# Block transposes of 32 by 32 on VectorE in place of TensorE transposes, in a hybrid attention layer

## The chip, the cores and the metric

The kernel runs on one core of one Trainium2 chip. The metric is the device time of one execution in microseconds; the time of a kernel is the median of its runs.

## The reference, cut to what matters

One layer over 2048 tokens of width 1024, all in float32, with RMS norms before and after each of three sub-layers:

```python
h = x
u = rms_norm(h, g_mix_pre)
z = u @ w_in                                   # sliding-window attention and a gated recurrence work on z
y = concatenate([ya, yh]) @ w_out
h = h + rms_norm(y, g_mix_post)
u = rms_norm(h, g_x_pre)
m = rms_norm(mem, g_mem)                       # 256 memory tokens
y = cross_attention(u, m, wq_x, wk_x, wv_x, wo_x)   # 4 heads, softmax over the memory tokens
h = h + rms_norm(y, g_x_post)
u = rms_norm(h, g_ffn_pre)
y = (silu(u @ w_gate) * (u @ w_up)) @ w_down
h = h + rms_norm(y, g_ffn_post)
```

## The kernel before, in words

Every large product is made from two float32r parts of each operand (a rounded part `hi` and the rest `lo = raw - hi`), so one product of 128x128 by 128x512 is three matmuls (lines 1122 to 1124 in `products`). Most products are also cut by Strassen's scheme: a block of two token tiles (2 x 128 tokens) by 1024 columns takes seven products in place of eight (`seven`), with sums and differences of the operands made on VectorE.

The middle of the kernel is `phases`, which runs a list of jobs (`jobs`). The first three are the output projection with the norms around it (`mixed_block`), the scores and the softmax of the cross-attention (`score_block`), and its values and output projection, folded into one matrix (`value_block`). Each has eight blocks, one for every two token tiles (n = 0, 2, ..., 14). After them come the FFN's jobs. Within a job the weights stay in SBUF as split tiles `T`; the tokens of a block are loaded from DRAM, transposed so that features lie on the partitions, by `streamed`, which splits them into tiles `S`. ScalarE makes `hi` and VectorE makes `lo` (`split2`, lines 985 and 988); the sums of the Strassen scheme come from `combine` (line 1097). `streamed` runs two products ahead of TensorE (`upto(need[g + 2])`).

A block is described by its stream, by `out` (what is done with each finished 128x512 part) and by `after`, a generator whose pieces are laid beside the steps of the next block, one piece a step. For a mixed block `after` scales the rows by the norm (line 1529), adds the residual rows x (line 1530), stores them to `h1_d`, takes the next norm's mean squares (line 1476), and then transposes both tiles on TensorE (`transposed`, lines 1381 and 1382: eight transposes of 128x128 into two PSUM banks, each bank copied out by ScalarE) and stores them to `h1t_d`. For a score block `out` makes the exponentials, and `after` divides them by their sums on VectorE (line 1573), transposes them in the same way and stores them to `pt_d`. A value block reads `pt_d` and also ends with transposes, of its own result, which go to `u_d`.

When a job nears its end, the weights of the next are fetched and split beside its last blocks (`half`, `resident`): these are the 128x1024 splits of line 988. Beside the blocks run sums of the weights of a later job (line 1032).

All loads and plain stores are issued by SyncE's queue (SP), in one order (`load`, line 75, and `store`, line 78). Row tiles come from a pool of 12 tiles of 128x1024 (`row_tile`); the raw streamed tiles (`sraw`) from a pool of four, two a block. The order within an engine's queue is set at build time by a scheduler that follows the order of the program's text and simulated times.

Of the kernel before, what the change touches and what calls it, by code (L numbers as in the profile page):

```python
# [11 lines left out]
F32 = mybir.dt.float32  # L12
F32R = mybir.dt.float32r
I32 = mybir.dt.int32
AF = mybir.ActivationFunctionType
# [3 lines left out]
P = 128  # L19
T = 2048  # L20
D = 1024
M = 256
# [7 lines left out]
NT = T // P  # L30
# [18 lines left out]
class Layer:  # L49
# [111 lines left out]
    def run(self):  # L161
        tc, nc, I = self.tc, self.nc, self.I
        self._n = 0
        self.last = {}
        kw = dict(reuse_waits="tile")
        self.z_d = tc.dram_tile([DIN, T], F32, name="z_d")

        self.y_d = tc.dram_tile([NT, P, D], F32, name="y_d")
        self.un_d = tc.dram_tile([KT, P, TB], F32, name="un_d")
        self.h1t_d = tc.dram_tile([NT, P, D], F32, name="h1t_d")  # L170
        self.pt_d = tc.dram_tile([NT, P, D], F32, name="pt_d")
        self.h1_d = tc.dram_tile([T, D], F32, name="h1_d")
        self.h2_d = tc.dram_tile([T, D], F32, name="h2_d")
        self.qk_d = tc.dram_tile([D, D], F32, name="qk_d")
        self.vo_d = tc.dram_tile([D, D], F32, name="vo_d")
        self.u_d = tc.dram_tile([KT, P, T], F32, name="u_d")
        self.h_d = tc.dram_tile([NFF, P, T], F32, name="hid_d")
        self.y2_d = tc.dram_tile([T, D], F32, name="y2_d")
        with (
            tc.tile_pool(name="cst", bufs=1) as self.cst,  # L180
            tc.tile_pool(name="sm", bufs=3, **kw) as self.sm,
            tc.tile_pool(name="edge", bufs=1, side="right") as edge,
        ):
            self.consts()

            for pool in (self.cst, edge):
                nc.gpsimd.memset(pool.tile([P, 24], F32, name="pad"), 0.0)
            with (
                tc.tile_pool(name="gp", bufs=1, **kw) as self.gp,
                tc.tile_pool(name="big", bufs=4, **kw) as self.big,  # L190
            ):
                self.mix()
# [867 lines left out]
        for e in (mybir.EngineType.Activation, mybir.EngineType.DVE):  # L1060
            self.last[e] = next((i for i in reversed(traced) if i.engine == e), None)

    def streamed(self, load, nk, kind, engine=None, tiles=False):


        nc = self.nc
        raw = []
        for j in range(2):
            self._n += 1
            t = self.ts.tile([P, 4, 256], F32, tag="raw", name=f"sraw_{self._n}", bufs=self.raws)  # L1070
            if tiles:
                t = t.rearrange("p k c -> p (k c)").rearrange("p (i c) -> p i c", i=2)
                load(t, j)
                raw.append([t[:, i, :].rearrange("p (k c) -> p k c", k=4) for i in range(2)])
            else:
                t = t[:, :nk, :]
                load(t, j)
                raw.append([t[:, :, i * P:(i + 1) * P] for i in range(2)])
        yield None
        (a11, a21), (a12, a22) = raw  # L1080

        room = []
        if kind == "u":
            t = self.tb.tile([P, 4, 2, 4, P], F32R, tag="T", name="S_u", bufs=3)
            room += [t[:, i] for i in range(4)]

        def made(src, e):
            self._n += 1
            t = room.pop(0) if room else self.ts.tile([P, 2, 4, P], F32R, tag="S", name=f"S_{self._n}", bufs=5)
            t = t[:, :, :nk, :]  # L1090
            self.split2(src, t[:, 0], t[:, 1], engine or e)
            return t

        def combine(a, b, op):
            self._n += 1
            t = self.st_pool.tile([P, 4, P], F32, tag="sum", name=f"sum_{self._n}", bufs=3)[:, :nk, :]
            nc.vector.tensor_tensor(t, a, b, op)
            return t

        if kind in "pqu":  # L1100
            for a, e in ((a11, "P"), (a21, "A"), (a12, "P"), (a22, "P")):
                yield made(a, e)
            return
        yield made(a11, "A")
        s1 = combine(a21, a22, ALU.add)
        yield made(s1, "P")
        s2 = combine(s1, a11, ALU.subtract)
        yield made(s2, "A")
        yield made(combine(a12, s2, ALU.subtract), "A")
        yield made(combine(a11, a21, ALU.subtract), "P")  # L1110
        yield made(a12, "A")
        yield made(a22, "P")
# [260 lines left out]
    def transposed(self, y, t):  # L1373
# [8 lines left out]
            nc.scalar.activation(tv[:, 4 * q:4 * q + 4, :], ps.rearrange("p (j t) -> p j t", j=4), AF.Copy)  # L1382
        return tv

    def store_transposed(self, dst, n, tv):
        self.store(dst[:, :, n * P:(n + 1) * P].rearrange("k p t -> p k t"), tv)

# [79 lines left out]
    def tokens(self, src, n):  # L1467

        return lambda kind: self.streamed(lambda t, j: self.load(
            t, src[n:n + 2, :, 512 * j:512 * j + 512].rearrange("i p c -> p i c")), 4, kind, "A", tiles=True)  # L1470

    def mean_square(self, a, to):

        self._n += 1
        junk = self.st_pool.tile([P, 512], F32, tag="part", name=f"junk_{self._n}", bufs=3)
        self.nc.scalar.activation(junk, a, AF.Square, scale=float(D) ** -0.5, accum_out=to)  # L1476
# [34 lines left out]
    def mixed_block(self, n):  # L1511
        nc = self.nc
        y, x, ss = {}, [], []
# [11 lines left out]
        def after():  # L1525
            r = self.rstds(ss[0])
            s2 = self.small("q_s", 4)
            for i in range(2):
                nc.vector.scalar_tensor_tensor(y[i], y[i], r[:, i:i + 1], self.g_mix_post, ALU.mult, ALU.mult)
                nc.vector.tensor_tensor(y[i], y[i], x[i], ALU.add)  # L1530
                self.store(self.h1_d[(n + i) * P:(n + i + 1) * P, :], y[i])
                yield
            yield
            for i in range(2):
                self.mean_squares(y[i], i, s2)
                yield
            r = self.rstds(s2)
            nc.gpsimd.tensor_scalar(self.r_x[:, n:n + 2], r, 1.0, None, ALU.mult)
            yield
            for i in range(2):  # L1540
                self.transposed(y[i], y[i])
                self.store(self.h1t_d[n + i], y[i])
                yield

        return self.tokens(self.y_d, n), out, after, None
# [1 line left out]
    def score_block(self, n):  # L1547
        nc = self.nc
        p, den = {}, {}
# [18 lines left out]
        def after():  # L1568
            for i in range(2):
                rd = self.small("mc", 4)  # L1570
                nc.vector.reciprocal(rd, den[i])
                for h in range(4):
                    nc.vector.tensor_scalar_mul(p[i][:, h * M:(h + 1) * M], p[i][:, h * M:(h + 1) * M], rd[:, h:h + 1])
                yield
            yield
            yield
            for i in range(2):
                self.transposed(p[i], p[i])
                self.store(self.pt_d[n + i], p[i])
                yield  # L1580

        return self.tokens(self.h1t_d, n), out, after, None

    def value_block(self, n):
        nc = self.nc
        y, ss, u, o = {}, [], {}, {}
# [41 lines left out]
                for i in range(2):  # L1628
                    yield from self.token_sums(u[i], o[i], n - 4 + i)

        return self.tokens(self.pt_d, n), out, after, None

    def hidden_blocks(self, b, f):
        nc = self.nc
# [130 lines left out]
```

## Time and profile before

| | us |
|---|---|
| median of 3 runs | 2568.96 |
| lowest, highest | 2566.59, 2569.04 |
| the profiled execution, its own time | 2568.82 |
| its span, from the first to the last instruction | 2566.8 |

In the views, PE is TensorE, PEld its weight loads, DVE VectorE, ACT ScalarE, POOL GpSimd and SP SyncE's DMA queue. A row of a group of instructions gives the line, engine and operation, what is written from what, the shapes, the count, the busy time in us and the mean duration in ns of one, and then the engine's idle time before them with what ended it. A row of a window gives, for each engine, the busy time in us and in brackets the number of instructions, then the granted TensorE clock as a share, the mean busy share of the 16 DMA engines (it passes 1 where packets wait for each other) and GB/s. A row of waits has the total in us, the count and the longest.

### The profile page before, as it was taken

What the parts mean: (1) busy time and instruction counts of PE and PEld (TensorE: products, weight loads), DVE (VectorE), ACT (ScalarE), POOL (GpSimd) and SP (SyncE); (2) the same over time, 40 slices, a digit from 0 to 9 for tenths busy, and PEclk for the clock granted to TensorE, in tenths of its full rate; (3) what the DMA queues carried; (4) which work ended last, traced back from release to release, by engine and by line L of the source; (5) the groups of instructions that cost most, each with busy time, mean ns of one, the idle gap of its engine ahead of it and who ended that gap; (6) DMA issues with size and microseconds to landing.
All of it is one profiled execution on the core that took longest, in us unless ns stands there. A gap on an engine that the chain in (4) does not pass through costs nothing.

```text
span 2566.8 us, 34858 instructions
## 1 busy us (share of the span) xinstructions
PE 2535.9 (99%) x12326; PEld 2125.3 (83%) x12326; DVE 1753.4 (68%) x2791; ACT 1298.0 (51%) x2715; POOL 358.1 (14%) x540
## 2 busy tenths in 40 slices
PE   9999999999999999999999999999999999999998
PEld 8888888888988888888878888888888888888886
DVE  7785488886556778687875655576666557574756
ACT  5563466665555676576663333353333335443543
POOL 4231334321301111101210000000000000000022
PEclk9999999999999999999999999999999999999999
DMA  6445755765887896666973622253565424464776
GB/s 189 148 164 170 200 164 166 231 197 163 259 280 276 300 323 206 214 214 210 331 246 115 205 91 79 79 204 124 182 201 190 156 99 178 171 190 107 228 173 156
DMA packets 357294, 486.35 MB, mean 189 GB/s; under 512 B 20352, under 2 KB 248704, under 8 KB 357120
## 3 DMA queue, kind: packets, MB, share of 16 engines
q1 hardware_dynamic: 351072, 462.11, 54.6%
q0 software_dynamic: 6048, 22.02, 4.9%
q8 instruction: 97, 1.59, 0.3%
q14 instruction: 77, 0.63, 0.1%
HBM read 317.34 MB, written 166.72 MB: 189 GB/s over the span
## 4 chain that ended last, share of the span: by engine, by line
PE 85%; DMA 5%; DVE 4%; ACT 2%; issue 2%; POOL 1%; SPq 0%; DVEq 0%; POOLq 0%; ACTq 0%
PE psm L1122 24%; PE psm L1123 23%; PE psm L1124 23%; PE psg L158 2%; PE psg L157 2%; PE psg L156 2%; PE pss L1381 1%; DMA u_d<-row 1%; DMA raw<-in_wo_x_dram 1%; DMA y_d<-sg 1%; DMA raw<-in_wv_x_dram 1%; DMA z<-in_w_out_dram 1%; DMA x<-in_w_out_dram 0%; DVE T L988 0%; DVE S L808 0%
## 5 line engine op out<-in xcount | busy, mean ns | idle before, releaser
L1123 PE MATMUL psm<-T,S 128*128 128x512 f32 x2680 | 1042.8, 390 | 1.2 <-DVE T L988 1.1
L1122 PE MATMUL psm<-T,S 128*128 128x512 f32 x2680 | 1036.5, 391 | 4.8 <-ACT part L1137 2.7
L1124 PE MATMUL psm<-T,S 128*128 128x512 f32 x2680 | 1030.0, 390 | 1.5 <-DVE S L988 1.5
L1122 PEld LDWEIGHTS psm<-T,S 128*128 128x128 f32 x2680 | 503.0, 188 | 113.4 <-ACT part L1137 5.6
L1124 PEld LDWEIGHTS psm<-T,S 128*128 128x128 f32 x2680 | 503.1, 188 | 107.3 <-DVE S L988 2.8
L1123 PEld LDWEIGHTS psm<-T,S 128*128 128x128 f32 x2680 | 503.2, 188 | 106.0 <-DVE T L988 3.4
L985 ACT ACTIVATE S<-sum 128x512 fp32r<-128x512 f32 (+1 forms) x370 | 223.7, 620 | 370.7 <-PE psm L1124 272.2
L988 DVE TENSOR_TENSOR S<-sraw,S 128x512 fp32r<-128x512 f32 (+1 forms) x315 | 211.5, 679 | 216.9 <-ACT S L985 213.7
L988 DVE TENSOR_TENSOR S<-sum,S 128x512 fp32r<-128x512 f32 (+1 forms) x388 | 259.5, 678 | 54.2 <-ACT S L985 49.1
L1137 ACT ACTIVATE part<-psm 128x512 f32<-128x512 f32 x285 | 169.1, 598 | 239.3 <-PE psm L1124 217.8
L985 ACT ACTIVATE S<-sraw 128x512 fp32r<-128x512 f32 (+1 forms) x300 | 185.2, 619 | 104.6 <-PE psm L1124 100.1
L1509 POOL DMA_DIRECT2D y_d<-row x16 | 14.1, 879 | 1077.4 <-DVE row L1695 1026.5
L988 DVE TENSOR_TENSOR T<-row,T 128x1024 fp32r<-128x1024 f32 (+1 forms) x112 | 131.3, 1187 | 41.1 <-ACT T L985 38.9
L157 PE MATMUL psg<-u,whi 128*128 128x512 f32 x320 | 127.8, 399 | 0.0
L158 PE MATMUL psg<-u,wlo 128*128 128x512 f32 x320 | 127.1, 397 | 0.0
L156 PE MATMUL psg<-u,whi 128*128 128x512 f32 x320 | 127.0, 397 | 0.0
L1476 ACT ACTIVATE junk<-row 128x512 f32<-128x512 f32 x160 | 99.7, 624 | 36.9 <-DVE row L1498 14.4
L985 ACT ACTIVATE T<-row 128x1024 fp32r<-128x1024 f32 (+1 forms) x112 | 113.7, 1034 | 6.1 <-DMA row<-d_s 3.3
L1646 DVE TENSOR_TENSOR row<-psm,part 128x512 f32<-128x512 f32 x66 | 43.7, 688 | 68.2 <-PE psm L1124 68.2
L1655 DVE TENSOR_TENSOR part<-psm,part 128x512 f32<-128x512 f32 x66 | 43.8, 688 | 60.4 <-PE psm L1124 60.2
L1695 DVE TENSOR_TENSOR row<-psm,part 128x512 f32<-128x512 f32 x72 | 49.1, 688 | 49.0 <-PE psm L1124 48.9
L812 ACT ACTIVATE S<-S,w_mn 128x256 f32<-128x256 f32 (+1 forms) x128 | 63.1, 497 | 34.3 <-DVE w_mn L808 34.0
(364 smaller groups left out, 3629.7 us busy)
## 6 DMA issues: line engine op xcount, KB each, us to landing
sraw<-in_w_gate_dram SPq DMA_DIRECT2D x44, 512.0 KB, 3.6
sraw<-in_w_up_dram SPq DMA_DIRECT2D x44, 512.0 KB, 3.7
hid_d<-row SPq DMA_DIRECT2D x44, 512.0 KB, 2.7
sraw<-hid_d SPq DMA_DIRECT2D x32, 512.0 KB, 3.9
sraw<-in_w_in_dram SPq DMA_DIRECT2D x44, 256.0 KB, 3.5
z_d<-pair SPq DMA_DIRECT2D x20, 512.0 KB, 2.9
raw<-in_w_in_dram SPq DMA_DIRECT2D x20, 512.0 KB, 4.9
z_d<-z SPq DMA_DIRECT2D x20, 512.0 KB, 3.9
```

The lines of the kernel that those rows point to most:

```text
L156: nc.tensor.matmul(ps, ah, bh, start=(i == 0), stop=False)
L157: nc.tensor.matmul(ps, ah, bl, start=False, stop=False)
L158: nc.tensor.matmul(ps, al, bh, start=False, stop=(i == n - 1))
L812: nc.scalar.activation(s[:, r, o:], s[:, r, o:], AF.Exp, bias=mn[:, i:i + 1], scale=-1.0, accum_out=den[:, i:i + 1])
L985: self.nc.scalar.activation(hi, raw, AF.Copy)
L988: self.nc.vector.tensor_tensor(lo, raw, f32(hi), ALU.subtract)
L1122: nc.tensor.matmul(ps, s[:, 0, k, :], t[:, 0, k, :], start=st, stop=False, **kw)
L1123: nc.tensor.matmul(ps, s[:, 0, k, :], t[:, 1, k, :], start=False, stop=False, **kw)
L1124: nc.tensor.matmul(ps, s[:, 1, k, :], t[:, 0, k, :], start=False, stop=sp, **kw)
L1137: nc.scalar.activation(t, ps, AF.Copy)
L1476: self.nc.scalar.activation(junk, a, AF.Square, scale=float(D) ** -0.5, accum_out=to)
L1695: nc.vector.tensor_tensor(d, a, b, ALU.add)
```

## The change

Three things are edited. The transposes of the mixed and score blocks leave TensorE and PSUM: `blocked` makes them with two VectorE instructions for a tile, each of which transposes the sixteen 32x32 blocks of a 128x512 half where they stand among the partitions, and writes into a new row tile. What is left of the transpose, the exchange of whole blocks between partitions, is done by the store: `store_blocked` writes each quarter of 32 partitions with a DMA of its own, 128 KB in pieces of 512 bytes, to its place in DRAM. So four stores take the place of one. The DRAM tiles `h1t_d` and `pt_d` have another shape, and the next job's `streamed` reads them with `blocked=True`: the loads have the same size, and the views that split and combine read are four-dimensional, with runs of 32 elements. The third edit moves the division of the probabilities from VectorE to ScalarE. The value blocks' own transposes stay on TensorE.

```diff
-        self.h1t_d = tc.dram_tile([NT, P, D], F32, name="h1t_d")
-        self.pt_d = tc.dram_tile([NT, P, D], F32, name="pt_d")
+        self.h1t_d = tc.dram_tile([NT, 2, P, 512], F32, name="h1t_d")
+        self.pt_d = tc.dram_tile([NT, 2, P, 512], F32, name="pt_d")
...
-    def streamed(self, load, nk, kind, engine=None, tiles=False):
+    def streamed(self, load, nk, kind, engine=None, tiles=False, blocked=False):
...
+        at = dict(a=4) if blocked else {}
+
+        def formed(t):
+            return t.rearrange("p k (a c) -> p k a c", **at) if blocked else t
+
...
-                raw.append([t[:, i, :].rearrange("p (k c) -> p k c", k=4) for i in range(2)])
+                raw.append([t[:, i, :].rearrange("p (a k c) -> p k a c" if blocked else "p (k c) -> p k c", k=4, **at)
+                            for i in range(2)])
...
-            self.split2(src, t[:, 0], t[:, 1], engine or e)
+            self.split2(src, formed(t[:, 0]), formed(t[:, 1]), engine or e)
...
+            t = formed(t)
             nc.vector.tensor_tensor(t, a, b, op)
...
+    def blocked(self, y):
+
+        t = self.row_tile()
+        for h in range(2):
+            hs = slice(h * 512, (h + 1) * 512)
+            self.nc.vector.transpose(t[:, hs].rearrange("p (b k j) -> p b k j", b=4, k=4),
+                                     y[:, hs].rearrange("p (k b i) -> p b k i", b=4, k=4))
+        return t
+
+    def store_blocked(self, dst, t):
+
+        for a in range(4):
+            self.store(dst[:, :, a * P:(a + 1) * P].rearrange("h (b i) s -> i (h b) s", b=4),
+                       t[a * 32:(a + 1) * 32, :].rearrange("i (g s) -> i g s", g=8))
+
...
+    def blocks(self, src, n):
+
+        return lambda kind: self.streamed(lambda t, j: self.load(
+            t, src[n:n + 2, j].rearrange("i p c -> p i c")), 4, kind, "A", tiles=True, blocked=True)
...
 # mixed_block
-                self.transposed(y[i], y[i])
-                self.store(self.h1t_d[n + i], y[i])
+                self.store_blocked(self.h1t_d[n + i], self.blocked(y[i]))
...
 # score_block
-                    nc.vector.tensor_scalar_mul(p[i][:, h * M:(h + 1) * M], p[i][:, h * M:(h + 1) * M], rd[:, h:h + 1])
+                    nc.scalar.activation(p[i][:, h * M:(h + 1) * M], p[i][:, h * M:(h + 1) * M], AF.Copy,
+                                         scale=rd[:, h:h + 1])
...
-                self.transposed(p[i], p[i])
-                self.store(self.pt_d[n + i], p[i])
+                self.store_blocked(self.pt_d[n + i], self.blocked(p[i]))
...
-        return self.tokens(self.h1t_d, n), out, after, None
+        return self.blocks(self.h1t_d, n), out, after, None
...
 # value_block
-        return self.tokens(self.pt_d, n), out, after, None
+        return self.blocks(self.pt_d, n), out, after, None
```

## The prediction

> **What bounds the kernel now.** I read the page first: the busy shares (its first part), and the chain of work that ended last.
>
> ```profile
> span 2566.8 us, 34858 instructions
> PE 2535.9 (99%) x12326; PEld 2125.3 (83%) x12326; DVE 1753.4 (68%) x2791; ACT 1298.0 (51%) x2715; POOL 358.1 (14%) x540
> ...
> PE 85%; DMA 5%; DVE 4%; ACT 2%; issue 2%; POOL 1%; SPq 0%; DVEq 0%; POOLq 0%; ACTq 0%
> ```
>
> TensorE is busy for 99% of the span and carries 85% of the chain. Taking TensorE work away shortens the kernel as long as the other engines keep up at the new pace. Whether they do has to be read from the two stages that the diff touches, the mixed blocks (about 789 to 955 us) and the score blocks (to about 1143 us). VectorE's timeline gives the period of a block: each mixed block has one pair on line 1529.
>
> ```profile
> 871.60 2.48 DVE L1529 SCALAR_TENSOR_TENSOR row<-row,q_r,g 128x1024 f32<-128x1024 f32 x2 [1.79 <-POOL q_r L1491]
> ...
> 892.45 2.48 DVE L1529 SCALAR_TENSOR_TENSOR row<-row,q_r,g 128x1024 f32<-128x1024 f32 x2 [1.79 <-POOL q_r L1491]
> ```
>
> So next I asked for busy time by windows of that period, 20.85 us, and for TensorE's waits from 780 to 1345 us.
>
> ```profile
> core 0: us, PE busy (x) PEld busy (x) DVE busy (x) ACT busy (x) POOL busy (x), PEclk, DMA share, GB/s
> 871.60:892.45 20.85, 20.85 (x101) 17.43 (x100) 15.80 (x20) 12.95 (x33) 2.49 (x7) 1.00 0.92 322
> 934.15:955.00 20.85, 20.85 (x101) 17.43 (x100) 18.85 (x20) 18.50 (x38) 3.42 (x7) 1.00 0.95 328
> 955.00:975.85 20.85, 20.85 (x100) 17.07 (x98) 17.35 (x23) 15.56 (x34) 3.15 (x6) 1.00 0.67 242
> 975.85:996.70 20.85, 20.85 (x99) 17.34 (x98) 19.53 (x38) 14.79 (x37) 4.54 (x6) 1.00 0.49 162
> 1017.55:1038.40 20.85, 20.85 (x101) 17.42 (x101) 15.68 (x30) 12.31 (x30) 4.11 (x5) 1.00 0.72 224
> 1220.00:1260.00 40.00, 38.49 (x181) 31.46 (x180) 36.43 (x50) 24.75 (x59) 9.67 (x12) 1.00 1.05 329
> ```
>
> ```profile
> PE psm L1124 <- DVE S L988: 1.5, 2, 1.2
> PE psm L1123 <- DVE T L988: 1.1, 2, 0.8
> PE psm L1122 <- ACT T L985: 0.5, 1, 0.5
> ```
>
> The first row is a steady mixed block, the fifth a steady score block; the second to fourth are the change from one job to the next, where the new weights are split. PE is full in all five, at a granted clock of 1.00, and those three waits of 3.1 us in all are the whole list. VectorE has 5.05 us free in the steady mixed block, but only 2.0, 3.5 and 1.3 us in the three at the change. DMA is at 0.92 of its engines in the mixed block. Those are the covers that the change draws on.
>
> **What leaves TensorE.** The transposes go through line 1381, with their copies out of PSUM on line 1382 (the view of one line, and the groups by line); the third view is TensorE's timeline around one tile of them (start, duration).
>
> ```profile
> L1381 PE MATMUL pss<-ident,row x384: 270/272/273, 811.4 to 1331.6; 128*128 128x128 f32 x192
> ...
> L1382 ACT ACTIVATE row<-pss 128x512 f32<-128x512 f32 x96 | 53.1, 594 | 2.1 <-PE pss L1381 1.5 <-DVE part L1655 0.4 <-ACT S L985 0.3
> ...
> 946.90 0.39 PE L1122 MATMUL psm<-T,S 128*128 128x512 f32 x1
> 947.13 0.39 PE L1123 MATMUL psm<-T,S 128*128 128x512 f32 x1
> 947.35 0.39 PE L1124 MATMUL psm<-T,S 128*128 128x512 f32 x1
> 947.58 1.03 PE L1381 MATMUL pss<-ident,row 128*128 128x128 f32 x8
> 948.38 0.48 PE L1122 MATMUL psm<-T,S 128*128 128x512 f32 x1
> 948.69 0.39 PE L1123 MATMUL psm<-T,S 128*128 128x512 f32 x1
> ```
>
> The 272 ns of one transpose is pipelined and not its cost; the starts tell that. Two product matmuls without a transpose start 0.23 us apart (946.90, 947.13, 947.35). From the start at 947.35 to the one at 948.69 lie two of them and the eight transposes: 1.34 - 2 x 0.23 = 0.88 us for a tile of eight. The 384 transposes are 48 tiles, 16 each of the mixed, score and value blocks; the value blocks keep theirs. So 32 tiles x 0.88 = **28.2 us** leave TensorE, all on the path, since PE has no idle time around them. The period of a block becomes 20.85 - 1.76 = 19.09 us. ScalarE loses 64 copies of 0.594 us, 2.38 us a block, off the path.
>
> **What VectorE gets.** The durations of its operations on these tiles, from the groups by line:
>
> ```profile
> L1498 DVE TENSOR_TENSOR row<-psm,part 128x512 f32<-128x512 f32 x21 | 14.4, 685 | 1.1 <-PE psm L1124 1.1
> ...
> L1573 DVE TENSOR_SCALAR row<-row,mc 128x256 f32<-128x256 f32 x64 | 18.4, 349 | 0.4
> ...
> L988 DVE TENSOR_TENSOR S<-sraw,S 128x512 fp32r<-128x512 f32 x50 | 34.0, 685 | 7.0 <-ACT S L985 6.8
> ```
>
> Each tile gets two block transposes of 128x512, four a block of two tiles. No transpose on VectorE stands in the trace. The nearest row of that size is 0.685 us (L1498), and I take it; the bounds are 0.35 us (the row of half the size) and twice the first, 1.37 us. Four cost 2.74 us a block. In the score blocks the eight divisions of 0.349 us leave, 2.79 us, so VectorE stays at 15.7 of 19.09 us there. In the steady mixed block it comes to 15.80 + 2.74 = 18.54 of 19.09 us, 97%: full, but still under TensorE. A block at 19.53 of 20.85 us (94%) went without a wait that shows in PE's busy time, because the split halves are made two products ahead. At the change of job it does not fit: 18.85 + 17.35 + 19.53 = 55.73 us in three blocks, with four transposes more in each of the first two (in the third the new four and the divisions cancel) 61.2 us, against 3 x 19.09 = 57.3. I charge the **3.9 us** over as a TensorE wait on line 988's splits; it is nothing if the two products of lead absorb it, and the place where it would be late next.
>
> The transposed tile is now stored in blocks, so the score and value blocks read it through views with runs of 32 elements, in seven VectorE operations a block (three splits, four differences). The trace shows no such run; the rows above have longer ones, all at 0.685 us. The cost lies between nothing and that price once more (a gain is excluded, since the same 512 elements are read), and I take nothing, because the rows above agree whether they read PSUM, a sum or the streamed tile. The upper end is a rival below. The Trainium skill ("Vector Engine (DVE) Microarchitecture Reference", section 5.2, Measured stream behaviour on trn2) has hops between runs of two or more adjacent words free, which would give the zero; no run here shows it.
>
> **What ScalarE gets.** The eight divisions of a score block. The two nearest rows:
>
> ```profile
> L985 ACT ACTIVATE S<-sum 128x384 fp32r<-128x384 f32 x32 | 16.8, 524 | 29.1 <-PE psm L1124 28.5 <-ACT S L985 0.6
> ...
> L985 ACT ACTIVATE S<-sum 128x512 fp32r<-128x512 f32 x338 | 207.0, 629 | 341.5 <-PE psm L1124 243.7 <-issue 96.3 <-ACT S L985 1.0
> ```
>
> 128 columns fewer save 105 ns, so 256 columns take about 0.42 us (between 0.35, VectorE's price, and 0.52): 8 x 0.42 - 2.38 = 1.0 us more, 13.3 of 19.09 us. What is queued behind them on ScalarE is line 985's halves; 5.8 us stay free. The transposes of these tiles come three steps after the divisions, about 8 us, so VectorE does not stand waiting for them.
>
> **What the DMA queue gets.** One store of 512 KB becomes four of 128 KB.
>
> ```profile
> L78 SPq DMA_DIRECT2D h1t_d<-row x16: 319/333/553, 822.0 to 976.7; - x16
> ...
> SPq L78 <- ACT row L1382: 62.9, 23, 7.5
> ...
> L78 SPq DMA_DIRECT2D u_d<-row x16: 360/388/870, 1171.0 to 1332.5; - x16
> ...
> DMA to landing us min/median/max: 3.2/6.4/10.6
> ...
> qd<-z_d SPq DMA_DIRECT2D x64, 128.0 KB, 3.4
> ```
>
> SP issues 3 x 32 = 96 instructions more, at 0.33 to 0.39 us (the rows of h1t_d and u_d): 2.0 to 2.3 us a block. SP already waits at these stores for the copies (62.9 us between 788 and 1142), and now waits for VectorE instead; the streamed loads stand behind, but they are issued a whole block ahead. The bytes do not change; at the shorter period the share of 0.92 becomes 0.92 x 20.85 / 19.09 = 1.00, below the 1.05 that the last window of the table reached. Charged at nothing, with the price if that cover is gone among the rivals.
>
> Sum: -28.2 + 3.9 = -24.3 us. The profiled execution took 2568.8 us (2.0 us outside its span), the median of the three is 2569.0; 2568.8 - 24.3 = 2544.5, which I give as **2545**.
>
> **The rivals.** *VectorE becomes the bound of the mixed blocks.* At 1.37 us a transpose a steady block there needs 15.80 + 5.48 = 21.3 us, so the mixed stage's 14.1 us are lost and 8 x 0.43 = 3.4 with them; the score block stays under 19.09 (15.68 - 2.79 + 5.48 = 18.4) and keeps its 14.1 less twice the 3.9: 2568.8 - 14.1 + 3.4 + 7.8 = 2566, and 2557 at 1.1 us. It decides from (19.09 - 15.80) / 4 = 0.82 us. For it: the block is left 0.55 us. Against: every plain 128x512 row lies at 0.685. The Trainium skill ("VectorE: DVE Perf Modes", The three transpose paths and its rules) has TensorE for a 128x128 transpose and gives VectorE 311 ns for 128 columns of bf16; four such would by estimate be 1.24 us, the side of this rival, where my sum has 0.685.
>
> *DMA becomes the bound of the mixed blocks.* Each of the new stores reads 32 partitions. If their packets take twice as long, then with 1.05 MB of a block's 322 GB/s x 20.85 us = 6.7 MB the share rises from 1.00 to 1.16; over 1.05 that stretches the block to 21.1 us, the mixed stage gains nothing and loses 2: about 2557. It decides from a price of 1.3 times (1.05). For it: the 0.92, and the 1.5 us that TensorE lost in the window at 1.05. Against: the loads have a block of lead, so a transfer can be late by most of 19 us unseen. The Trainium skill ("SBUF — State Buffer", Door 1: The DMA port swizzle) says that 32 partitions reach 8 of 16 ports, 189 GB/s against 328 at 1 MiB; this speaks against the change, on the side of this rival.
>
> *Slower: the four stores wait for one another.* Their pieces interleave in one DRAM tile. If each waited on SP for the one before to land, three waits of 3.4 us (the 128 KB row) a tile, 20.4 us a block, come on SP's own issuing (some twenty DMAs a block at 0.33 to 0.39, 7 us): 27.4 us against 20.85, and 16 blocks are longer by 6.5: 2568.8 + 104 = 2673. It decides from a landing of (20.85 - 7) / 6 = 2.3 us. For it: the least landing in the row above is 3.2 us. Against it: the stores to u_d interleave in the same way, and the list of SP's waits from 1160 to 1345 us has no store that waits for one of them.
>
> *Slower: the blocked views are read at double price.* 7 x 0.685 = 4.8 us more puts the score block at 20.5 us, 1.4 over 19.09, and a value block, by the fullest window of the table (36.43 of 40 us, 19.0 a block), at 23.8, 2.95 over 20.85: 8 x (1.4 + 2.95) = 35 us, 2579. It starts to cost from (20.85 - 19.0) / 7 = 0.26 us an operation and turns the sign from about 0.6. For it: the value blocks have little room. Against: the equal prices of the rows.
>
> *The work does not leave the path*: the new lead is eaten by lateness of the splits in both stages, within 5 us of 2569.
>
> **Numbers.** What a measurement of this kernel can tell from no change is about 0.2%, 5 us. Chances: forecast 0.62, VectorE bound 0.12 (2546 at 0.82 us to 2566; three quarters of it over 0.2% faster), DMA bound 0.07, stores that wait 0.08, blocked views 0.05, no effect 0.06. Faster: 0.62 + 0.09 + 0.07 = 0.78; same: 0.03 + 0.06 = 0.09; slower: 0.08 + 0.05 = 0.13. The range begins at 2539, just under the sum without the 3.9 (2540.6), and ends at 2563, which takes in the DMA rival, most of the VectorE one and, beside the forecast, a lateness of the splits that is five times as large as charged; the two slower cases and the one without effect, 0.19, lie outside.
>
> **What would show it.** Right: 128 transposes left on line 1381, none before the value blocks; L1529 pairs about 19.1 us apart; 64 VectorE transposes near 0.69 us; VectorE over 95% busy in the mixed blocks; a few us of TensorE waiting on line 988 between about 920 and 980 us. Wrong: transposes over 0.82 us, streamed splits of the score blocks slower than 0.69 us, waits of line 78 on a DMA into h1t_d or pt_d, or a DMA share at 1.05 with TensorE idle in the mixed blocks.

## The result: 2559.7 us, and the profile after

The changed kernel takes 2559.66 us (median of 10 runs, 2553.22 to 2564.53) beside 2568.32 for the kernel before (10 runs); the ratio is 0.9965, with an interval of 0.9957 to 0.9974. It is faster by 8.7 us where 24.3 were forecast. The page of its profile, the first lines and the chain:

```profile
span 2559.0 us, 34405 instructions
PE 2511.9 (98%) x12070; PEld 2101.6 (82%) x12070; DVE 1769.1 (69%) x2791; ACT 1293.2 (51%) x2715; POOL 362.7 (14%) x540
...
PE 77%; DMA 9%; DVE 7%; issue 3%; ACT 3%; SPq 1%; POOL 1%; DVEq 0%; POOLq 0%; ACTq 0%
```

TensorE is busy 24.0 us less, but the span is shorter by only 7.8. The rest became idle time of TensorE, and its share of the chain went from 85% to 77%. The waits of TensorE between 780 and 1345 us (total, times, longest), which were 3.1 us before:

```profile
PE psm L1129 <- ACT part L1144: 7.8, 4, 6.1
PE psm L1131 <- DVE S L988: 3.9, 4, 1.3
PE psm L1130 <- DVE T L988: 3.4, 5, 1.4
PE psm L1129 <- ACT S L985: 2.7, 2, 1.7
```

They are 17.8 us now, and the longest waits for ScalarE. (Lines 1129 to 1131 are the three product matmuls, 1144 the copy of a product out of PSUM, 1388 the transposes, 1397 `blocked`, 1556 and 1587 to 1599 what were 1529 and 1561 to 1573.) The operations that the change adds, from the groups by line, and then what is left of these transposes on TensorE, from the view of that line (none before 1160 us). A VectorE instruction of line 1397 takes a 128x512 half, which is sixteen 32x32 blocks in each of its four groups of 32 partitions, 64 in all:

```profile
L1397 DVE STREAM_TRANSPOSE row<-row 128x512 f32<-128x512 f32 x64 | 40.7, 681 | 0.4 <-ACT row L1599 0.3
L1599 ACT ACTIVATE row<-row,mc 128x256 f32<-128x256 f32 x64 | 27.1, 502 | 0.0
```

```profile
L1388 PE MATMUL pss<-ident,row x128: 271/273/273, 1160.0 to 1323.0; 128*128 128x128 f32 x128
```

The splits of the blocked views, in the groups of the score job (980 to 1110 us):

```profile
L988 DVE TENSOR_TENSOR S<-sraw,S 128x512 fp32r<-128x512 f32 x19 | 12.9, 682 | 2.5 <-ACT S L985 2.2
```

The unit prices are those of the forecast: a transpose 0.681 us, a split of a blocked view 0.682. A division reads 0.502 alone, but four in a row take 1.71 us (below). Windows of the changed kernel: three blocks of the mixed job by its pairs on line 1556, a piece of the score job, its end, the stretch in which TensorE waits, and the one behind it.

```profile
core 0: us, PE busy (x) PEld busy (x) DVE busy (x) ACT busy (x) POOL busy (x), PEclk, DMA share, GB/s
831.22:850.64 19.42, 18.44 (x81) 14.63 (x80) 17.72 (x25) 11.17 (x27) 2.99 (x7) 1.00 0.85 299
850.64:871.18 20.54, 20.54 (x92) 17.04 (x91) 18.60 (x25) 11.83 (x28) 4.13 (x7) 1.00 0.97 324
871.18:890.50 19.32, 18.41 (x81) 14.93 (x81) 17.30 (x25) 10.65 (x26) 3.73 (x7) 1.00 1.00 338
1030.00:1049.00 19.00, 19.00 (x86) 15.58 (x85) 12.68 (x22) 10.65 (x28) 1.98 (x3) 1.00 0.73 209
1090.00:1109.00 19.00, 17.71 (x79) 14.34 (x78) 16.25 (x23) 17.32 (x40) 4.61 (x4) 1.00 1.01 305
1109.47:1118.20 8.73, 2.76 (x13) 1.95 (x11) 6.64 (x9) 8.73 (x19) 0.00 (x0) 0.91 0.57 226
1118.00:1124.00 6.00, 5.71 (x15) 4.51 (x16) 3.93 (x5) 3.93 (x7) 0.00 (x0) 0.55 0.30 81
```

In the mixed job VectorE is 90 to 91% busy, and TensorE loses a microsecond in two of the three blocks. (The share alone does not decide: in the kernel before, VectorE was busy for 18.85 and 19.53 of 20.85 us in two of the windows tabled, 90 and 94%, and TensorE lost nothing.) In the steady score block nothing is lost. At the end of the score job ScalarE is busy for 17.32 of 19 us, then for 8.73 of 8.73, while TensorE works for 2.76; then TensorE runs at a granted clock of 0.55.

**A ledger by place.** Every kernel here has 8040 of these product matmuls in the same order, so the same matmul can be looked up by its number in two traces. How much earlier it starts than in the profile of before is the lead. What a stretch adds to the lead leaves out the time that was lost ahead of it, though a wait that is carried over a border is not excluded. The stretches: *early*, up to the first mixed block (product 504, 794.6 us before); *A*, to product 1260 (981.5), which holds the 16 tiles of the mixed job; *B*, to 1680 (1086.7), eleven tiles of the score job; *C*, to 1932 (1149.9), its last five and the start of the value job; *rest*. At 0.88 us a tile, 14.1, 9.7 and 4.4 us leave TensorE in A, B and C. Leads in us, each from one profile:

```
                                          early      A      B      C   rest
what leaves TensorE                         -     14.1    9.7    4.4    -
changed kernel, three profiles            0.6    4.5    9.2   -5.2   -1.4
                                          1.6    3.3    9.3   -4.9    0.0
                                         -1.0    4.3    9.3   -5.5   -0.4
division on VectorE, three profiles       4.0    4.4   10.0    1.5   -1.2
                                         -2.8    3.7    8.3    1.7   -3.3
                                          0.1    4.3    9.5    0.2   -2.2
no VectorE transposes                    -1.1   11.0    9.6   -0.8   -3.1
one store a tile                          1.4    7.8    9.5   -4.0   -0.4
no transposes, one store                 -4.1   13.9    9.0    1.7   -2.6
four stores, long runs                   -1.0    2.3   10.0   -3.6    0.3
division, two a step                      1.9    1.4    8.5   -4.5   -2.0
transposes in halves, division VectorE   -1.8    5.1    8.7    0.7   -2.7
both of these, division ScalarE          -7.2    5.2    9.1   -4.4   -2.9
division on both engines                 -0.6    4.9    5.5    0.2   -3.2
last two blocks' division on VectorE     -1.0    3.0    9.4   -0.9   -2.9
division VectorE, no row addition        -0.9   11.1    9.8   -2.1   -1.8
division VectorE, row addition GpSimd    -4.6   -6.5   10.0    1.5   -2.5
division both, row addition GpSimd       -1.0   -6.3    5.0    2.6   -2.6
division VectorE, row addition by DMA     1.2  -23.1   10.0    1.3   -3.3
```

The early column is before anything that was edited. It runs from -7.2 to 4.0, and over 6.8 us for one and the same kernel, so a single profile or median cannot tell a difference of a few us in these stages; A, B and C repeat within 1.8 us in the kernels that were profiled three times. The changed kernel keeps nearly all of B (9.2 to 9.3 of 9.7), 3.3 to 4.5 of 14.1 in A, and in C it loses 5 us instead of gaining 4.

### The profile page after: what moved, and what is told of

Same layout as the page of the kernel before. It is cut to its first block, busy times and chain, and to the rows that moved or that the text cites. A ratio compares the mean times of both kernels' runs of the same rounds, so it can differ in the third digit from the quotient of the medians.

```text
span 2559.0 us, 34405 instructions
## 1 busy us (share of the span) xinstructions
PE 2511.9 (98%) x12070; PEld 2101.6 (82%) x12070; DVE 1769.1 (69%) x2791; ACT 1293.2 (51%) x2715; POOL 362.7 (14%) x540
## 3 DMA queue, kind: packets, MB, share of 16 engines
q8 instruction: 95, 1.56, 0.2%
## 4 chain that ended last, share of the span: by engine, by line
PE 77%; DMA 9%; DVE 7%; issue 3%; ACT 3%; SPq 1%; POOL 1%; DVEq 0%; POOLq 0%; ACTq 0%
PE psm L1129 21%; PE psm L1131 21%; PE psm L1130 21%; PE psg L158 2%; PE psg L156 2%; PE psg L157 2%; DVE S L988 1%; DVE T L988 1%; DMA x<-in_w_out_dram 1%; DMA pt_d<-row 1%; DMA g<-vo_d 1%; DMA row<-d_s 1%; DMA y_d<-sg 1%; ACT T L985 1%; DMA z<-in_w_out_dram 1%
```

## The experiments

**Undoing one part each.** Four kernels against the change: `e1` puts line 1599 back on VectorE; `e2` stores the row without transposing it; `e3` writes one store a tile; `e4` does the last two. In the last three the blocks of a tile are not, or not fully, transposed, so the score and value blocks work on other numbers with the same instructions.

```diff
 # e1
-                    nc.scalar.activation(p[i][:, h * M:(h + 1) * M], p[i][:, h * M:(h + 1) * M], AF.Copy,
-                                         scale=rd[:, h:h + 1])
+                    nc.vector.tensor_scalar_mul(p[i][:, h * M:(h + 1) * M], p[i][:, h * M:(h + 1) * M], rd[:, h:h + 1])
 # e2, in blocked
-        t = self.row_tile()
-        ...
-        return t
+        return y
 # e3, in store_blocked
+        self.store(dst.rearrange("h p s -> p h s"), t.rearrange("p (h s) -> p h s", h=2))
```

> The changed kernel with the divisions by the sums put back on VectorE; all else as changed. Three theories of where about 20 us of the 28.2 us that left TensorE went. ScalarE theory: the moved divisions stand in ScalarE's order ahead of the copies and splits that TensorE needs, above all at 1112 us, where TensorE loses 8.7 us: this run takes about 2551 us, and that gap is gone. VectorE theory: the block transposes overfill VectorE, so 2.8 us more of it in each score block makes it worse: 2560 to 2566 us. Store theory (four stores instead of one delay the loads behind them): 2560 us, unchanged.

> The changed kernel without the 64 VectorE transposes: the untransposed rows are stored by the same four stores, so the output is not the layer's. VectorE theory: nearly all of the loss goes, 2541 to 2546 us. ScalarE theory: the gaps of the mixed stage may go, the 8.7 us at the change from score to value blocks stay: 2549 to 2556 us. Store theory: 2557 to 2560 us, as changed.

> The changed kernel with one store of 512 KB for each transposed tile in place of four of 128 KB, without the exchange of blocks between partitions, so the output is not the layer's; VectorE transposes and divisions as changed. Store theory: 2542 to 2550 us. VectorE and ScalarE theories: 2557 to 2560 us, as changed.

> The changed kernel without the VectorE transposes and with one store for each tile: what is left of the change is that TensorE no longer transposes, that the divisions are on ScalarE, and the blocked views of the reads; the output is not the layer's. If VectorE and the stores are the whole loss: 2540 to 2543 us (2568.3 less 28.2). ScalarE theory: 2548 to 2553 us, with the gap at the change from score to value blocks still there.

Ratios to the kernel before: e1 0.9918 [0.9901, 0.9936], e2 0.9918 [0.9902, 0.9935], e3 0.9932 [0.9916, 0.9949], e4 0.9895 [0.9874, 0.9916]. The kernel before took 2575.0 us beside these four, so the times that were expected are read as ratios to 2568.3: e1 then agrees with the ScalarE theory (0.993), e2 falls between two theories, e3 lies near the store theory (0.990 to 0.993), and e4, with all divisions still on ScalarE, comes out as if VectorE and the stores were the whole loss (0.989 to 0.990). Each part costs something, and the ledger says where: the division 5 to 7 us in C and nothing in A; the transposes about 7 us in A (11.0 against 4.0, the mean of three) and 4.4 in C; the four stores some 3 us in A (7.8 against 4.0, and 13.9 against 11.0). With neither transposes nor four stores, A gains 13.9 of 14.1, which confirms the 0.88 us a tile.

What happens in C, in ScalarE's timeline of the changed kernel (start, duration):

```profile
1110.57 2.96 ACT L985 ACTIVATE T<-row 128x1024 fp32r<-128x1024 f32 x3
1113.42 1.71 ACT L1599 ACTIVATE row<-row,mc 128x256 f32<-128x256 f32 x4
1115.01 0.63 ACT L985 ACTIVATE S<-sum 128x512 fp32r<-128x512 f32 x1
1115.53 0.63 ACT L985 ACTIVATE S<-sraw 128x512 fp32r<-128x512 f32 x1
1116.05 1.71 ACT L1599 ACTIVATE row<-row,mc 128x256 f32<-128x256 f32 x4
1117.65 0.59 ACT L1144 ACTIVATE part<-psm 128x512 f32<-128x512 f32 x1
```

and in e1, at the same work:

```profile
1103.23 2.96 ACT L985 ACTIVATE T<-row 128x1024 fp32r<-128x1024 f32 x3
1106.09 0.62 ACT L985 ACTIVATE S<-sum 128x512 fp32r<-128x512 f32 x1
1106.60 0.62 ACT L985 ACTIVATE S<-sraw 128x512 fp32r<-128x512 f32 x1
1107.12 0.58 ACT L1144 ACTIVATE part<-psm 128x512 f32<-128x512 f32 x1
```

From the three weight splits (the value job's) to the copy on line 1144 is 7.08 us in the first and 3.89 in the second; the difference of 3.2 us is the two lots of four divisions. That copy empties the product bank that TensorE needs next. TensorE's timeline of the changed kernel at that matmul and the two behind it:

```profile
1118.29 0.79 PE L1129 MATMUL psm<-T,S 128*128 128x512 f32 x1 [6.06 <-ACT part L1144]
1118.88 0.63 PE L1130 MATMUL psm<-T,S 128*128 128x512 f32 x1
1119.31 0.63 PE L1131 MATMUL psm<-T,S 128*128 128x512 f32 x1
```

It stands for 6.06 us, and the next matmuls start 0.43 us apart instead of 0.23. In e1 the same matmul waits 1.21 us. But in e4 it waits only 0.54 us, with the same divisions on ScalarE, and C comes out as in e1 (1.7). ScalarE's timeline of e4 there (line 1592 is the division):

```profile
1104.41 0.58 ACT L1144 ACTIVATE part<-psm 128x512 f32<-128x512 f32 x1
...
1106.37 1.70 ACT L1592 ACTIVATE row<-row,mc 128x256 f32<-128x256 f32 x4
1107.97 0.58 ACT L1144 ACTIVATE part<-psm 128x512 f32<-128x512 f32 x1
```

Without the VectorE transposes this queue has another order: one lot of four divisions, not two, stands between this copy and the one on line 1144 before it. So the divisions alone do not make the gap; it takes the VectorE transposes as well, or the order of ScalarE's queue that comes with them.

**Order or amount.** Is it that four divisions or two transposes stand in a row? `e6` issues two divisions in each of four steps; `e7` is e1 with one half of a tile transposed in each step; `e8` does both with the division on ScalarE; `e5` is the changed kernel beside them.

```diff
 # e6, e8
                 for h in range(4):
                     nc.scalar.activation(..., AF.Copy, scale=rd[:, h:h + 1])
+                    if h % 2:
+                        yield
-                yield
-            yield
-            yield
 # e7, e8, in blocked, which becomes a generator
                                      y[:, hs].rearrange("p (k b i) -> p b k i", b=4, k=4))
+            if not h:
+                yield
```

> The changed kernel as it is, beside the next three on one chip. All theories: ratio 0.9955 to 0.9975 to the kernel before, about 9 us; ScalarE busy without a gap from about 1109 to 1118 us, with a TensorE gap of about 6 us there.

> The divisions stay on ScalarE, the same eight a block at the same cost, but two in each of four steps instead of four in each of two. ScalarE theory, by order (four in a row, 1.7 us, stand ahead of the split and the copy that TensorE waits for): the gap at 1112 us shrinks from 6 to under 2 us, and the kernel gains 5 to 8 us on the changed one. ScalarE theory, by amount (ScalarE is simply full at the change of job): the same eight divisions still stand ahead, and it gains under 2 us. VectorE and Store theories: under 2 us, since neither queue is touched.

> Division back on VectorE as in the first experiment, and the two transposes of a tile in two steps, one half in each, instead of both in one; the four stores as in the change. VectorE theory, by order (1.3 us in a row ahead of a sum or a split): the gaps of 1.9 and 1.1 us at about 822, 843, 884 and 945 us shrink, and it gains 3 to 6 us on the first experiment, ratio near 0.990. VectorE theory, by amount (97% full): the lateness only moves, within 2 us of the first experiment, 0.992. Store theory: no change to the first experiment.

> Both spreadings, the division on ScalarE. If order decides for both engines: 0.988 to 0.990 and the fastest of all with the whole result, since in the score blocks it keeps 2.8 us of VectorE a block free that the seventh fills. If amount decides on ScalarE: no better than the changed kernel by more than the transposes give, 0.994 to 0.996.

Ratios: e5 0.9951 [0.9935, 0.9966], e6 0.9960 [0.9945, 0.9975], e7 0.9938 [0.9921, 0.9955], e8 0.9972 [0.9962, 0.9982]. Spreading brings nearly nothing back: C stays at -4.5 and -4.4 with the divisions spread, and A at 5.1 with the transposes spread. The one long gap becomes two shorter ones (2.7 and 2.0 us in e6). So it matters little whether they stand in a row. e8 came out a little above all that was expected of it.

That is not yet an answer for amount against order, since the order of a queue is set anew with each build, and the edits change it. The longest wait of the mixed job shows this. TensorE's line of the changed kernel, and ScalarE's timeline ahead of it (line 1527 copies a finished product out of PSUM):

```profile
825.77 0.50 PE L1129 MATMUL psm<-T,S 128*128 128x512 f32 x1 [1.72 <-ACT S L985]
```

```profile
824.09 0.60 ACT L1527 ACTIVATE row<-psm 128x512 f32<-128x512 f32 x1 [2.04 <-PE psm L1131]
824.58 0.62 ACT L985 ACTIVATE S<-sum 128x512 fp32r<-128x512 f32 x1
825.10 0.62 ACT L985 ACTIVATE S<-sraw 128x512 fp32r<-128x512 f32 x1
```

The same in e2 (line 1522 is the same copy):

```profile
823.67 0.62 ACT L985 ACTIVATE S<-sum 128x512 fp32r<-128x512 f32 x1
824.20 0.62 ACT L985 ACTIVATE S<-sraw 128x512 fp32r<-128x512 f32 x1
825.80 0.60 ACT L1522 ACTIVATE row<-psm 128x512 f32<-128x512 f32 x1 [0.99 <-PE psm L1131]
```

In the changed kernel ScalarE is not full here: it sits idle for 2.04 us before a copy that waits for TensorE, and the two splits that TensorE needs next stand behind that copy. In e2 they stand ahead of it. The 13 profiles of kernels with the transposes and the residual addition on VectorE all have the first order and this wait, e7 with its spread transposes too; before, e2, e4, e10, e11, e13 and e15 have the second order. Of these, before and e4 do not wait there, and the others wait for a split on VectorE (0.47 us in e2, 1.56 in e13), two matmuls on.

**The amount on ScalarE.** `e9` leaves the even heads' divisions on ScalarE and gives the odd ones to VectorE; `e14` leaves the first six blocks' on ScalarE and gives those of the last two (`n >= NT - 4`) to VectorE.

> Of the four divisions of a score tile two stay on ScalarE and two go back to VectorE. ScalarE theory, by amount (ScalarE is full at the change from the score to the value job, the sixth run having shown that two a step lose as much as four): half of what the first experiment recovered, some 4 us on the changed kernel, or all of it if what is left fits; ratio 0.991 to 0.994, and the gap of 6 us at 1112 under 4. A theory in which any division on ScalarE at all delays the split by one place would leave the gap as it is: 0.995 to 0.996.

> The changed kernel with the divisions of the last two of eight score blocks on VectorE, those of the first six on ScalarE. ScalarE theory, by amount at the change of job: the gap of 6 us at 1112 goes, and the kernel comes to the first experiment, 0.991 to 0.993. If ScalarE's divisions cost in every score block: it recovers about a quarter, 0.995.

Ratios 0.9956 [0.9941, 0.9971] and 0.9966 [0.9951, 0.9980]. By the ledger both do in C about what was expected, 0.2 and -0.9 against -5.2 (in e14 a gap of 2.6 us is left of the 6). But neither shows in the time: e9 loses 4 us in B, in one place because a split stands on ScalarE behind four exponentials and two divisions (TensorE idle for 2.12 us), and e14 stands 1 us lower in A and 2 us lower in the rest. So C follows the number of divisions that ScalarE has at the end of the score job, as long as the transposes are on VectorE, and in their totals both are misses: what is recovered at the end of the score job is in part taken back in the value job (the rest is -1.2 to -3.3 in the kernels whose C is above -3, and 0.3 to -1.4 in those that lost it, e6 and e8 apart). What waits there has not been taken apart.

**The amount on VectorE.** The residual addition of the mixed blocks, two of 1.21 us a block, is nearly what the transposes brought. `e10` gives it to GpSimd, `e11` does so to e9, `e13` leaves it out, and `e15` does it with an accumulating DMA; e10, e13 and e15 start from e1. `e16` is e1 again.

```diff
 # e10, e11 (mixed_block)
-                nc.vector.tensor_tensor(y[i], y[i], x[i], ALU.add)
+                nc.gpsimd.tensor_tensor(y[i], y[i], x[i], ALU.add)
 # e15
-                nc.vector.tensor_tensor(y[i], y[i], x[i], ALU.add)
-                self.store(self.h1_d[(n + i) * P:(n + i + 1) * P, :], y[i])
+                self.add(y[i], self.I["x"], n + i)
...
             for i in range(2):
+                self.store(self.h1_d[(n + i) * P:(n + i + 1) * P, :], y[i])
                 self.mean_squares(y[i], i, s2)
```

> The first experiment (division on VectorE) with one thing more: the addition of the residual to the row in the mixed blocks, two of 1.21 us a block, goes from VectorE to GpSimd, which is busy for 3 to 4 us of 19. VectorE theory, by amount: what the transposes brought (2.6 us a block) is nearly taken away again, so the mixed stage gains 4 to 6 us as it did without the transposes, ratio 0.989 to 0.991. If it is not the amount but the place of the transposes ahead of a sum that costs, the gaps at about 820, 842 and 882 us stay, and it is within 2 us of the first experiment, 0.992. Were GpSimd and VectorE to slow one another, it would be above that.

> The two before this together. If both amounts count, the two gains add: 0.988 to 0.990, the fastest with the whole result. If not, no better than the better of the two.

> The first experiment (division on VectorE) without the addition of the residual to the row in the mixed blocks, two of 1.21 us a block (the addition is left out). VectorE theory, by amount: 2.4 of the 2.74 us a block that the transposes brought are off VectorE again, so the mixed stage loses as little as without transposes, 4 to 6 us less than the first experiment. By place (the transposes stand ahead of a sum, whatever is left out elsewhere): within 2 us of the first experiment.

> The first experiment with the residual added by an accumulating DMA from the input instead of a load and an addition on VectorE; the two halves of the block's chain stand two steps further apart, to leave time for it. VectorE theory, by amount: 2 to 6 us faster than the first experiment, unless ScalarE's sums of squares wait for the DMA (then TensorE waits on line 985 by as much). By place: within 2 us, or slower by the DMA's landing.

> The first experiment again, for comparison on one chip: 0.990 to 0.993.

Ratios: e10 0.9995 [0.9985, 1.0005], e11 1.0006 [0.9996, 1.0015], e13 0.9927 [0.9911, 0.9943], e15 1.0038 [1.0023, 1.0053], e16 0.9944 [0.9929, 0.9960]. In e13, with the transposes where they were, but 2.4 us a block less on VectorE, A gains 11.1, as without the transposes (11.0), where e1 and its repeats gain 4.1. So it is not the place of the transposes; taking as much other work off VectorE does the same. e13 also has the second of the two orders above on ScalarE, so how much of its gain is less work and how much that order was not separated. A window of e13, and the same one of e16:

```profile
890.00:910.00 20.00, 20.00 (x90) 16.57 (x89) 14.19 (x20) 11.40 (x27) 2.91 (x7) 1.00 0.92 264
```

```profile
890.00:910.00 20.00, 18.71 (x82) 15.13 (x82) 17.77 (x24) 11.36 (x27) 3.54 (x7) 1.00 0.91 281
```

The first has VectorE at 71% and 90 matmuls in 20 us, the second at 89% and 82. e10, e11 and e15 moved the work and made it worse, each in its own way; the gain that was hoped for came in none. e16 missed its expectation, above the 0.990 to 0.993 expected: in their profiles e1 was 4.0 us ahead, and e16 2.8 us behind, before the edited code begins. GpSimd's timeline of e10, and VectorE's:

```profile
880.04 6.18 POOL L1557 TENSOR_TENSOR row<-row,row 128x1024 f32<-128x1024 f32 x2 [2.33 <-DVE row L1556]
```

```profile
881.07 2.89 DVE L988 TENSOR_TENSOR S<-sraw,S 128x512 fp32r<-128x512 f32 x1
883.90 3.40 DVE L1032 TENSOR_TENSOR extra<-extra,row 128x1024 f32<-128x1024 f32 x1
887.22 0.68 DVE L988 TENSOR_TENSOR S<-sum,S 128x512 fp32r<-128x512 f32 x1
```

While GpSimd adds, a split of 0.69 us takes 2.89 and an addition of 1.22 takes 3.40; the next, when GpSimd is done, takes 0.68 again. In e15 it is SP's queue (its waits, 790 to 1020 us):

```profile
SPq L78 <- DMA row<-in_x_dram: 51.9, 13, 16.3
```

The store of the row waits on SP until the addition has landed, and the streamed loads stand behind it: A loses 23 us.

**The four stores.** `e12` keeps them but writes two runs of 2 KB in each partition instead of eight of 512 bytes, at rows where the readers do not look for them.

> The changed kernel with its four stores a tile of 32 partitions each, but every partition is written as two runs of 2 KB instead of eight of 512 bytes (the rows then lie where the score and value blocks do not expect them; the arithmetic stays as it is). Store theory, by issues (SP's four instructions and their four waits a tile): as the changed kernel, 0.995. Store theory, by the size of the pieces: as with one store of 512 KB, which has runs of 2 KB too, 0.992 to 0.993.

0.9956 [0.9939, 0.9972], and A is 2.3: as the changed kernel, not as one store. By these single profiles it is the number of stores, not the size of the pieces. SP's queue of the changed kernel shows what four do, in its timeline and in its waits from 790 to 970 us:

```profile
862.57 3.97 SPq L78 DMA_DIRECT2D h1t_d<-row  x5
...
868.47 2.14 SPq L78 DMA_DIRECT2D h1t_d<-row  x3
870.71 0.42 SPq L75 DMA_DIRECT2D sraw<-y_d  x1
```

```profile
SPq L78 <- DMA row<-in_x_dram: 6.0, 7, 1.4
SPq L78 <- DMA row<-in_w_out_dram: 2.6, 4, 0.8
SPq L78 <- DMA row<-qk_d: 2.5, 4, 0.9
```

Eight stores take 6.1 us of SP before the streamed load can be issued at 870.71. Stores wait for the landing of loads with which they share no data, 11 us in these three rows; in the same list of the kernel with one store a tile, no store waits for a load. That these waits, rather than the issuing itself, are the 3 us in A was not separated.

**The change with and without its third edit, side by side.**

> The changed kernel beside the next one: 0.995 to 0.997 to the kernel before by all theories, as it was twice.

> Division on VectorE, the rest as changed. ScalarE theory: 0.991 to 0.994, its interval below that of the changed kernel. If the divisions cost nothing in all (what they lose at the change of job is waited for anyway at the start of the value blocks): the same ratio as the changed kernel.

The changed kernel 0.9965 [0.9953, 0.9978], with the division on VectorE 0.9940 [0.9928, 0.9953]: 2562.1 and 2555.5 us. The change without its third edit is the better version, by some 6 us. No kernel here that computes the whole layer is clearly faster (e7, which differs in the spread transposes, has 0.9938).

## Why the prediction was wrong in size and right in direction

**Right: 28.2 us leave TensorE**, all on the path. Where nothing else was late, the lead came out as counted: 13.9 of 14.1 in A with neither transposes nor four stores, and up to 10.0 for 9.7 in B. **Right: the prices**, 0.681 for 0.685 a transpose, nothing for the blocked views, 1.71 us for four divisions against 4 x 0.42. The rivals of the blocked views, of stores that wait for one another's landing, and of the slow transpose fell with them: no wait of a store on a DMA into h1t_d or pt_d shows, and the transposes stay under 0.82. The DMA rival fell too: the DMA share in the three mixed blocks is 0.85 to 1.00, under 1.05, and e2, with the same four stores a tile, gains 11.0 of 14.1 in A.

**Wrong: "full, but still under TensorE".** The step compared sums, 18.54 against 19.09 us a block, and charged nothing for the last 3%. The splits are a chain between ScalarE and VectorE with two products of lead; with four transposes more, single ones come late before the block's sum is full, and one order of ScalarE's queue puts two of them behind a copy that waits for TensorE. TensorE lost 10 us in A (14.1 less 4.0), some 7 of them with the transposes on VectorE (11.0 without), where 3.9 were charged, and those at the change of job only. There the waits on line 988 came to 2.0 us (1.4 and 0.5, at 961 and 958 us). "VectorE over 95% busy" was wrong too: it is 90 to 91% with TensorE already losing a microsecond in a block. VectorE as the bound was a rival, but with a point from which it decides of 0.82 us a transpose; it cost these 7 us at 0.68. How much of them is VectorE's amount, and how much the changed order on ScalarE, stays open.

**Wrong: the divisions on ScalarE, "5.8 us stay free".** That is the steady score block, and there it held (B loses half a microsecond). The step did not look at the end of the score job, where ScalarE splits the value job's weights. Before's windows there:

```profile
1108.00:1127.00 19.00, 19.00 (x97) 15.96 (x97) 15.59 (x28) 15.47 (x33) 1.46 (x4) 1.00 0.72 249
1127.00:1137.00 10.00, 10.00 (x50) 8.36 (x49) 8.86 (x12) 9.46 (x18) 0.00 (x0) 1.00 0.51 170
```

At 15.47 of 19 us, and then at 9.46 of 10 where the changed kernel later stands for 6 us, the rows would have said that little or nothing is free there. The prediction had tabled such windows at the first change of job and not at the second. C came out at -5.2 where the five tiles should have given 4.4: 9.6 us, nearly as much as in A. It takes both engines: without the transposes (C -0.8, and 1.7 in e4) or without the divisions (0.2 to 1.7) most of it goes, so the step that failed is ScalarE's cover at the change of job together with the transposes' effect on it. What in the pair makes it, the work or the order of ScalarE's queue, is not shown.

**Wrong: the four stores "charged at nothing".** About 3 us, in A. The named cover, a block of lead, was not enough on a queue where the stores stand ahead of the streamed loads; by which wait the 3 us reach TensorE was not followed, and none in its list above is put down to a load.

In sum: 28.2, less 10.1 in A, 0.4 in B, 9.6 in C and 0.6 in the rest, with 0.4 gained early (means of the three profiles of the changed kernel), is 7.9; their spans are shorter by 7.8, 9.3 and 6.6. The range held the time because it had been drawn to take in the VectorE rival and splits five times as late as charged; the loss at the end of the score job was in none of the cases, and that the time still fell inside is luck.

## What to carry to other kernels

A share of busy time does not say whether an engine that feeds the busiest one is free: here VectorE cost TensorE time at 90%, and in the kernel before it cost none at 94%. In the waits that were followed here the late step stood behind something else in its queue, so read what stands ahead of the steps, before and after: a small edit on one engine can change the order on another. Look up every stage change for each engine that gets work, not only the steady block and not only the first change. And compare kernels by the lead of the same instruction in two traces: a total that moves by several us before the edited code begins hides a few us in it.

## What the runs showed of the hardware

TensorE's clock can fall behind a gap, and not always behind the same one. All kernels with the transposes and the residual addition on VectorE have an idle time of 1.72 us in the first mixed blocks, for the same split; 13 profiles show it. In six the five to eight matmuls behind it start 0.40 to 0.46 us apart, in seven none does. The same window behind that gap, of the changed kernel and of e18:

```profile
826.00:830.00 4.00, 3.64 (x10) 2.57 (x10) 2.33 (x3) 1.82 (x5) 1.12 (x3) 0.57 1.09 348
```

```profile
826.00:830.00 4.00, 3.34 (x13) 2.47 (x14) 1.78 (x3) 2.35 (x6) 1.12 (x3) 1.00 1.05 342
```

The granted clock is 0.57 in one and 1.00 in the other. Behind the nine gaps of 4.7 to 6.7 us in all the profiles it fell every time (five to twelve matmuls 0.43 us apart instead of 0.23, up to 2.4 us more). The Trainium skill ("TensorE: Matmul & The Clock Gate", What's actually happening) has half the clock after an idle window of about 3.4 us that runs freely. That one and the same gap brings it in some profiles and not in others would fit a window whose phase is chance, which no run here measures; but 1.72 us were enough in six of 13 profiles, so here the length on the page does not hold. The Trainium skill ("SBUF — State Buffer", Who interferes with whom) has a VectorE instruction with two SBUF inputs contend with a GpSimd instruction that reads SBUF. e10's 2.89 us for 0.69 agrees with it.
